# One level of Strassen on the first quarter's value product, with whole weights kept beside the rounded ones and a new order of the work

## The chip, the cores and the metric

The kernel runs on one core of one Trainium2 chip. The metric is the device time of one execution in microseconds (us); the times given are medians over runs. TensorE multiplies matrices (its instructions are called PE below, its weight loads PEld), VectorE (DVE) and ScalarE (ACT) do the elementwise work, and SyncE (SP) issues nearly all transfers between the chip's memory (DRAM) and the on-chip memory.

## The reference

The kernel computes one decoder layer over 2048 tokens of width 1024, in float32. What concerns the change is the cross-attention into 256 memory tokens with 4 heads:

```python
h = rms_norm(x, xa_norm_g[l])
m = rms_norm(mem, mem_norm_g[l])
q = (h @ w_q[l]).reshape(bsz, s, XA_HEADS, XA_HD)
kv = m @ w_kv[l]
k, v = jnp.split(kv, 2, axis=-1)
...
p = jax.nn.softmax(scores, axis=-1).astype(v.dtype)
o = jnp.einsum("bhsm,bmhd->bshd", p, v).reshape(bsz, s, d)
x = x + o @ w_o[l]
```

Before it stand a mixer (an input projection, a gated recurrence, a convolution over 31 positions, an output projection `w_out`), and behind it a feed-forward part with `w_up` and `w_down` and a last norm.

## The kernel before, in words

**Rounded pairs.** Every float32 factor of a large product is split into a rounded part `hi` and a rest `lo` (`split`: ACT writes `hi`, DVE subtracts to get `lo`), and every product is three matmuls of 128 rows by 512 columns (`mm3`: hi·hi, hi·lo, lo·hi) that add up in one PSUM bank.

**Folded memory.** The memory tokens are folded into weights once: `memory_a` makes A (keys times `w_q`, 1024 by 4·256) and `memory_vo` makes VO (values times `w_o`, 4·256 by 1024). Each is written to DRAM as hi and lo (`keep`), in blocks of 128 rows by 512 columns, and later read back block by block (`Rows.get`). So for a token the scores are one product with A and the attention's output is one product of the 1024 probabilities with VO: the latter is the **value product**.

**Quarters.** The tokens go in four quarters of 512. `attend(q)` does quarters 0 and 1 one by one: output projection with `w_out`, scores, softmax, value product (`project_tokens(PT, VO_rows, ...)`: for each half of the output columns, 8 blocks of the probabilities' columns times 4 blocks of 128 tokens, 3 matmuls each). Before the value product the probabilities are turned (128 by 128 transposes on TensorE) and split, into the tiles `pth` and `ptl`. Quarters 2 and 3 are done together by `attend_pair`, whose three products use one level of Strassen's algorithm over 1024 tokens (`Folded`): the left factor is cut into A11, A12 (first 512 tokens, first and second half of the columns) and A21, A22; the weight into B11 to B22; seven products of half the size stand for eight. `Folded.STEPS` lists them. Some use sums: S1 to S4 of the left blocks (made by DVE as they are needed, tiles `s`) and T1 to T4 of the weight's blocks. The T's are made ahead by `fold_weights`, which runs `Folds.prepare` for `w_out`, A and VO in this order and writes them to DRAM (`t_out`, `t_a`, `t_vo`); for A and VO each block is first put together again from its hi and lo by one DVE addition (`wd<-wh,wl`). In `Folded` the split left blocks are the tiles `hidh` and `hidl`, the same names that the feed-forward's down product uses.

**Order.** The program is recorded by Python generators (tasks) that a driver steps by a clock of estimated TensorE time; `TURNS` ranks them, the conditions in `NORMED`, `ATTEND` and `FOLD_AT` gate them, and some thirty numbers (`MIX_WAIT`, `ATT_PACE`, `FOLD_PACE` ...) delay them. `Program.schedule` then orders the recorded instructions of each engine by due times that come from estimated durations and from a transfer rate `DMA_RATE`; on-chip tiles come from 84 slots of 128 by 512 (`SLOTS`), granted in the order of recording. On the chip every engine runs its own list in that fixed order and waits on semaphores, and SP issues its transfers in its list's order. All instructions carry one line (399), so the profile is read by tile names. Of a DRAM tensor the name's number can differ between the two programs (VO_90 and VO_91 are the same tensor).

Of the kernel before, what the change touches and what calls it, by code (L numbers as in the profile page):

```python
# [11 lines left out]
F32 = mybir.dt.float32  # L12
F32R = mybir.dt.float32r
AF = mybir.ActivationFunctionType
ALU = mybir.AluOpType
# [37 lines left out]
DMA_DELAY = 2.5  # L53
DMA_RATE = 300e3
ACT_SWITCH = 1.3
# [367 lines left out]
def hybrid_layer(  # L423
# [519 lines left out]
    def keep(rows, k, half, cols, src):  # L943

        base = (k * 2 + half) * 2
        for i in range(2):
            tok = rows.kept.tok.setdefault(base + i, Buf(None, (1,)))
            pr.dma(rows.kept.at(base + i)[:, cols], src[i].f32(), writes=[tok], join=True)

    def memory_a():  # L950
# [50 lines left out]
        for h in range(4):  # L1001
# [20 lines left out]
    def memory_vo():  # L1022
        yield mem_a
        yield VO_LATE
        for h in range(4):
# [203 lines left out]
    def normed(q, ready, wait):  # L1229
# [6 lines left out]
        mixed[q] = Y, L  # L1236

    def attend(q, ready):
        for t in ready:
# [23 lines left out]

        yield from turned(xs, take)
        turned_x[q].done = True
        yield mem_a
        prob = [[], []]

        def soft(tb, half, p):
            prob[half].append(softmax(p, rp[:, tb : tb + 1], rn[:, tb : tb + 1]))  # L1270

        yield from project_tokens(X, A_rows, soft, None, ATT_PACE[q][1])
        del X
        PT = []
        yield VO_WAIT
        turn_p(prob[0], PT)
        yield mem_vo
        st2 = Stats()

        def add2(tb, half, p):  # L1280
            V("tensor_tensor", xs[tb][half][:], xs[tb][half][:], p[:], op=ALU.add)
            st2.add(tb, half, xs[tb][half][:])
            x2_kept.put((q * NTB + tb) * 2 + half, xs[tb][half][:])

        yield from project_tokens(PT, VO_rows, add2, lambda: turn_p(prob[1], PT), ATT_PACE[q][2])
        attended[q].done = True
        del PT
        r2 = st2.rstd()
# [23 lines left out]
    def combine(name, a, b, op):  # L1312
        t = tmp(name)
        V("tensor_tensor", t[:], a, b, op=op)
        return t
# [322 lines left out]
    class Folds:  # L1638
# [41 lines left out]
    class Folded:  # L1680
# [3 lines left out]

        def __init__(self, src, folds, add):
            self.src, self.folds, self.put, self.s = src, folds, add, {}

# [16 lines left out]
        def gather(self, n):  # L1704
            akey, bkey = self.STEPS[n]
            L, R = [], []
            for i in range(KH):
                src = self.operand(akey, i)
                hi, lo = pair("hid")
# [252 lines left out]
    EARLY, VO_WAIT, V_LATE, Z_COPIED = 5, 2, 500, (0, 1)  # L1962
    MIX_WAIT, MIX_TURN, LN_SUM, LN_SQ, GATES = (5, 7, 6, 0), 5, 6, 0, 3
    MIX_PACE, ATT_PACE = (1, 4, 3, 4), ((0, 3, 0), (0, 2, 2), (6, 3, 3), (5, 9, 0))
    PAUSE, WARM = 2, 16
    FED = ("B21", "T2", "T1", "T3")
    MEM_WAIT, VO_LATE, ATT_TURN, FFN_TURN, X_PACE, T_PACE = 17, 10, 1, (3, 8, 7, 24), 3, 10

    FOLDED = (2, 3)
    PAIR_WAIT, PAIR_TURN, FOLD_PACE = (0, 0, 9, 17), 7, (6, 7, 35)  # L1970
# [4 lines left out]
    NORMED = [lambda: ([m[0]], 108), lambda: ([attended[0]], 31), lambda: ([m[2]], 26), lambda: ([m[3], n[2]], 6)]  # L1975
    ATTEND = [lambda: [n[0]], lambda: [n[1]]]
    TURNS = lambda: [later, first, fold, m[0], mem_a, m[1], first_t, a[0], n[2], m[3], n[0], n[3], mem_vo, n[1], m[2], a[1], a[2], tail]
    X = [HalfX(h) for h in range(NH)]
# [70 lines left out]
```

## Time and profile before

| | |
|---|---|
| median of 3 runs | 2402.87 us (2400.91 to 2404.35) |
| profiled execution: its time / its span | 2401.64 us / 2399.8 us |
| PE / PEld busy | 99% / 82% of the span |
| DVE / ACT busy | 85% / 55% |
| DMA | 604.56 MB, mean 252 GB/s |

A busy PE means that a matmul was in flight; matmuls overlap, so their rate is read from how many start in a stretch. A group's row gives the busy time of its instructions (overlaps counted once) and the mean duration of one; then the idle time of the engine just before them and who ended it.

### The profile page before, as it was taken

How to read it: one execution, taken by the hardware profiler on the slowest of the kernel's cores; microseconds unless marked ns; L12 is line 12 of the kernel's file. 1: busy time of each engine (PE TensorE's matmuls, PEld its weight loads, DVE VectorE, ACT ScalarE, POOL GpSimd, SP SyncE). 2: the span in 40 equal slices, each digit the busy share in tenths (PEclk: the TensorE clock that was granted, in tenths of full speed). 3: DMA queues.
4: the chain of work that ended last, by engine and by line, in shares of the span. 5: the costliest groups of instructions: out<-in, count | busy, mean ns of one | idle time of the engine just before them, and what ended most of it. 6: DMA issues, size and time to landing. Idle time of an engine off the chain costs nothing.

```text
span 2399.8 us, 33427 instructions
## 1 busy us (share of the span) xinstructions
PE 2385.4 (99%) x10940; PEld 1977.0 (82%) x10940; DVE 2034.9 (85%) x3353; ACT 1319.6 (55%) x2380; POOL 0.7 (0%) x6
## 2 busy tenths in 40 slices
PE   9999999999999999999999999999999999999998
PEld 8798888888887888888888888888888888888887
DVE  6999995299899869879999887988988896777787
ACT  7782676357557778695555555554555541222333
POOL 0000000000000000000000000000000000000000
PEclk9999999999999999999999999999999999999999
DMA  9688788775878988787766544556565599887986
GB/s 308 220 297 314 241 298 301 255 263 175 289 261 272 322 275 273 277 284 268 253 231 205 199 171 158 174 177 211 192 215 199 184 308 321 283 280 253 315 299 255
DMA packets 364434, 604.56 MB, mean 252 GB/s; under 512 B 35371, under 2 KB 117547, under 8 KB 364260
## 3 DMA queue, kind: packets, MB, share of 16 engines
q1 hardware_dynamic: 364108, 602.16, 73.3%
q8 instruction: 86, 1.41, 0.2%
q14 instruction: 88, 0.72, 0.1%
q10 hardware_dynamic: 152, 0.28, 0.0%
HBM read 409.36 MB, written 192.94 MB: 251 GB/s over the span
## 4 chain that ended last, share of the span: by engine, by line
PE 84%; DVE 9%; ACT 3%; DMA 2%; issue 1%; SPq 0%; DVEq 0%; ACTq 0%
PE ps L399 84%; DVE conv L399 4%; DMA h<-hid 1%; DMA wl<-w_down 1%; ACT L399 1%; DVE wl L399 1%; DVE hidl L399 0%; DVE s L399 0%; DVE acc L399 0%; ACT gate L399 0%; DVE al L399 0%; ACT junk L399 0%; DMA wl<-w_in 0%; DVE xc L399 0%; DVE xl L399 0%
## 5 line engine op out<-in xcount | busy, mean ns | idle before, releaser
L399 PE MATMUL ps<-Xh,wh 128*128 128x512 f32 x1344 | 523.5, 390 | 0.7 <-ACT u L399 0.7
L399 PE MATMUL ps<-Xh,wl 128*128 128x512 f32 x1344 | 523.4, 389 | 0.7 <-DVE wl L399 0.5
L399 PE MATMUL ps<-Xl,wh 128*128 128x512 f32 x1344 | 523.2, 389 | 0.0
L399 PE MATMUL ps<-wh,hidl 128*128 128x512 f32 x960 | 374.4, 390 | 1.0 <-DVE hidl L399 1.0
L399 PE MATMUL ps<-wh,hidh 128*128 128x512 f32 x960 | 374.5, 390 | 0.8 <-ACT hidh L399 0.8
L399 PE MATMUL ps<-wl,hidh 128*128 128x512 f32 x960 | 373.8, 389 | 0.0
L399 DVE SCALAR_TENSOR_TENSOR conv<-cb,v,conv 128x512 f32<-128x512 f32 x480 | 337.1, 755 | 2.2 <-ACT conv L399 1.4
L399 PEld LDWEIGHTS ps<-Xh,wl 128*128 128x128 f32 x1344 | 252.4, 188 | 53.6 <-DVE wl L399 1.5
L399 PEld LDWEIGHTS ps<-Xh,wh 128*128 128x128 f32 x1344 | 252.4, 188 | 53.1 <-ACT u L399 1.1
L399 PEld LDWEIGHTS ps<-Xl,wh 128*128 128x128 f32 x1344 | 252.4, 188 | 52.4
L399 ACT ACTIVATE hidh<-s 128x512 fp32r<-128x512 f32 x186 | 113.8, 631 | 271.1 <-DVE s L399 232.6
L399 PEld LDWEIGHTS ps<-wh,hidl 128*128 128x128 f32 x960 | 180.3, 188 | 40.2 <-DVE hidl L399 3.1
L399 PEld LDWEIGHTS ps<-wh,hidh 128*128 128x128 f32 x960 | 180.3, 188 | 38.3 <-ACT hidh L399 1.3
L399 PEld LDWEIGHTS ps<-wl,hidh 128*128 128x128 f32 x960 | 180.3, 188 | 37.1
L399 PE MATMUL ps<-xh,wh 128*128 128x512 f32 x512 | 204.6, 400 | 0.5 <-DVE vol L399 0.5
L399 PE MATMUL ps<-xh,wl 128*128 128x512 f32 x512 | 200.4, 391 | 0.0
L399 PE MATMUL ps<-xl,wh 128*128 128x512 f32 x512 | 200.1, 391 | 0.0
L399 ACT ACTIVATE wh<-s 128x512 fp32r<-128x512 f32 x192 | 119.5, 629 | 116.7 <-DVE s L399 82.0
L399 ACT ACTIVATE wh<-raw 128x512 fp32r<-128x512 f32 (+2 forms) x214 | 127.9, 613 | 54.2 <-PE ps L399 22.7
L399 ACT ACTIVATE u<-ps 128x512 f32<-128x512 f32 x144 | 85.7, 595 | 129.1 <-PE ps L399 128.2
L399 DVE TENSOR_TENSOR wl<-raw,wh 128x512 fp32r<-128x512 f32 (+2 forms) x214 | 141.5, 675 | 14.7 <-ACT wh L399 13.7
L399 DVE TENSOR_TENSOR acc<-acc,ps 128x512 f32<-128x512 f32 (+1 forms) x157 | 103.4, 682 | 59.2 <-PE ps L399 55.3
(241 smaller groups left out, 4029.9 us busy)
## 6 DMA issues: line engine op xcount, KB each, us to landing
raw<-in_w_up_dram SPq DMA_DIRECT2D x96, 512.0 KB
wh<-w_down SPq DMA_DIRECT2D x156, 256.0 KB
wl<-w_down SPq DMA_DIRECT2D x156, 256.0 KB
w_down<-wh SPq DMA_DIRECT2D x144, 256.0 KB
w_down<-wl SPq DMA_DIRECT2D x144, 256.0 KB
h<-hid SPq DMA_DIRECT2D x120, 256.0 KB
wh<-w_in SPq DMA_DIRECT2D x96, 256.0 KB
wl<-w_in SPq DMA_DIRECT2D x96, 256.0 KB
```

What stands on the lines that cost most here:

```text
L399: getattr(e, name)(*[resolve(a) for a in args], **{k: resolve(a) for k, a in kw.items()})
```

## The change

1. `attend(0)` does its value product by `Folded` on halves of 256 tokens (`HALVED = ((), (0,))`; the first tuple, for the scores, is empty). The turned probabilities are copied unsplit (tiles `pt`); S1 to S4, the splits and the seven products are 256 tokens wide, with 2 blocks of tokens in place of 4.
2. `memory_a` and `memory_vo` write the whole float32 blocks too (`split_kept`: one more ACT copy, tiles `aw` and `vow`, and one more transfer each, to `A2w` and `VO2w`), and `Folds.block` reads these in place of hi, lo and an addition.
3. `fold_weights` runs VO first, as soon as `memory_vo` is done, then `w_out`, then A.
4. `DMA_RATE` in the planner is 320e3 in place of 300e3, and the numbers that delay and rank the tasks are others.

```diff
-DMA_RATE = 300e3
+DMA_RATE = 320e3
...
+            self.whole = None if w is not None else Kept(name + "w", n * 2, F32)
...
+        tok = rows.whole.tok.setdefault(k * 2 + half, Buf(None, (1,)))
+        pr.dma(rows.whole.at(k * 2 + half)[:, cols], src[2], writes=[tok], join=True)
+
+    def split_kept(name, p):
+        t = *pair(name), tmp(name + "w")
+        split(p[:], *t[:2])
+        ACT(t[2][:], p[:], AF.Copy)
+        return t
...
-                t = pair("a")
-                split(p[:], *t)
+                t = split_kept("a", p)
...
-                t = pair("vo")
-                split(p[:], *t)
+                t = split_kept("vo", p)
...
+    def in_halves(src, kq, tiles):
+        for th in range(2):
+            src[th, kq] = [t[:, th * TT // 2 : (th + 1) * TT // 2] for t in tiles]
...
+        if q in HALVED[1]:
+            src = {}
+
+            def turn_half(half):
+                tiles = []
+                for j in range(4):
+                    p = ps()
+                    with together():
+                        for tb in range(NTB):
+                            transpose(p[:, tb * P : (tb + 1) * P], prob[half][tb][:, j * P : (j + 1) * P], ident[:])
+                    t = tmp("pt")
+                    ACT(t[:], p[:], AF.Copy)
+                    tiles.append(t)
+                in_halves(src, half, tiles)
+
+            turn_half(0)
+            yield mem_vo
+            yield F_vo.done
+
+            def before(n):
+                if n == 1:
+                    turn_half(1)
+                yield 0
+
+            def put(th, tb, half, bank, last):
+                add2(th * NTB // 2 + tb, half, bank, last)
+
+            yield from Folded(src, F_vo, put, TT // 2).run(before, at_once)
+            del src
+        else:
...
-            hi, lo = self.rows.get(k, half)
-            t = tmp("wd")
-            V("tensor_tensor", t[:], hi[:].f32(), lo[:].f32(), op=ALU.add)
-            return t
+            return self.rows.whole.get(k * 2 + half, None, "wd")
...
-            for tb in range(NTB):
+            for tb in range(self.width // P):
...
-        for f, ready, wait in zip((F_out, F_a, F_vo), FOLD_AT(), FOLD_PACE):
+        for f, ready, wait in zip((F_vo, F_out, F_a), FOLD_AT(), FOLD_PACE):
...
-    MIX_WAIT, MIX_TURN, LN_SUM, LN_SQ, GATES = (5, 7, 6, 0), 5, 6, 0, 3
+    MIX_WAIT, MIX_TURN, LN_SUM, LN_SQ, GATES = (4, 3, 2, 0), 9, 6, 0, 3
...
+    HALVED = ((), (0,))
-    FOLD_AT = lambda: ([turned_x[0]], [mem_a, turned_x[1]], [mem_vo])
+    FOLD_AT = lambda: ([mem_vo], [turned_x[0]], [mem_a, turned_x[1]])
```

The lists of the engines show what moves. First DVE at quarter 0's value product. Before, the splits of the turned probabilities (`ptl`) stand among a few sums of the `w_out` fold, and then come the additions of the finished banks to the tokens (`x_...`, one tile for each block of 128 tokens and half of the columns):

```order
L399 TENSOR_TENSOR ptl<-ps,pth 128x512 x4
L399 TENSOR_TENSOR t<-wd 128x512 x2
L399 TENSOR_TENSOR t<-wd,t 128x512 x2
L399 TENSOR_TENSOR ptl<-ps,pth 128x512 x4
L399 TENSOR_TENSOR x_2909<-x_2909,ps 128x512
L399 TENSOR_TENSOR x_2929<-x_2929,ps 128x512
L399 TENSOR_TENSOR x_2946<-x_2946,ps 128x512
```

Now, at the same place, from the splits of A12 (the first row) over the sums of the third product:

```order
L399 TENSOR_TENSOR hidl<-pt,hidh 128x256 x4
L399 TENSOR_TENSOR t<-wd 128x512
L399 TENSOR_TENSOR t<-wd,t 128x512
L399 TENSOR_TENSOR s<-pt 128x256
L399 TENSOR_TENSOR s<-s,pt 128x256
L399 TENSOR_TENSOR x_3035<-x_3035,ps 128x512
L399 TENSOR_TENSOR x_3040<-x_3040,ps 128x512
L399 TENSOR_TENSOR s<-pt 128x256 x2
L399 TENSOR_TENSOR s<-s,pt 128x256 x2
L399 TENSOR_TENSOR hidl<-s,hidh 128x256
```

Sums of 256 columns (`s`), splits of them (`hidl`) and fold sums of `w_out` (`t`) now stand between the additions to the tokens; further down the same list come 16 splits `wl<-t_vo,wh` of the T's.

Next, SP's list inside the value product. Before, it reads VO's hi and lo (`wh`, `wl`), with the fold of `w_out` in between (`wd` read, `t_out` written):

```order
L399 DMA wh<-VO_90 128x512
L399 DMA wl<-VO_90 128x512
L399 DMA wd<-in_w_out_dram 128x512
L399 DMA wh<-VO_90 128x512
L399 DMA wl<-VO_90 128x512
L399 DMA t_out<-t 128x512
L399 DMA wh<-VO_90 128x512
L399 DMA t_out<-t 128x512
```

Now, behind the first two products' blocks:

```order
L399 DMA wl<-VO_91 128x512
L399 DMA wd<-in_w_out_dram 128x512
L399 DMA t_out<-t 128x512 x2
L399 DMA t_vo<-t_vo 128x512 x3
L399 DMA t_out<-t 128x512
L399 DMA x_93<-x_3035 128x512
L399 DMA t_vo<-t_vo 128x512
L399 DMA wd<-in_w_out_dram 128x512 x2
```

The fold of `w_out` is still in between; the T's are read back (`t_vo<-t_vo`), and finished tokens are already written (`x_93`). On PE the place reads, before, with turns of probabilities (`ident,prob`) among the products:

```order
L399 MATMUL ps<-wh,ptl 128x512
L399 MATMUL ps<-ident,prob 128x128 x8
L399 MATMUL ps<-wh,pth 128x512
L399 MATMUL ps<-wl,pth 128x512
L399 MATMUL ps<-wh,ptl 128x512
L399 MATMUL ps<-wh,pth 128x512
```

and now, with all turns ahead and the value product in one piece:

```order
L399 MATMUL ps<-xl,wh 128x512
L399 MATMUL ps<-xh,wl 128x512
L399 MATMUL ps<-ident,prob 128x128 x16
L399 MATMUL ps<-wh,hidh 128x512
L399 MATMUL ps<-wl,hidh 128x512
L399 MATMUL ps<-wh,hidl 128x512
```

From there 168 such matmuls follow each other without another task's work; before there were 192, with 16 turns among them. The last 5833 instructions of PE's list, the feed-forward part, are the same in both programs.

More of the change, by code (lines that the diff above doesn't have):

```diff
@@ L1262, in take, with take_raw @@
             X.append((hi, lo))
-        yield from turned(xs, take)
+        def take_raw(k, p):
+            t = tmp("xa")
+            ACT(t[:], p[:], AF.Copy, scale=vec["v1024"][:, k, G_XA : G_XA + 1])
+            X.append(t)
+        yield from turned(xs, take_raw if q in HALVED[0] else take)
         turned_x[q].done = True
         yield mem_a
-        prob = [[], []]
+        prob = [{}, {}]
         def soft(tb, half, p):
-            prob[half].append(softmax(p, rp[:, tb : tb + 1], rn[:, tb : tb + 1]))
@@ L1272, in attend, with soften @@
-        yield from project_tokens(X, A_rows, soft, None, ATT_PACE[q][1])
+            prob[half][tb] = softmax(p, rp[:, tb : tb + 1], rn[:, tb : tb + 1])
+        if q in HALVED[0]:
+            score = {}
+            def soften(th, tb, half, bank, last):
+                at = (th * NTB // 2 + tb, half)
+                if not last:
+                    t = score[at] = tmp("score")
+                    ACT(t[:], bank[:], AF.Copy)
+                    return
+                t = score.pop(at)
+                V("tensor_tensor", t[:], t[:], bank[:], op=ALU.add)
+                soft(*at, t)
+            yield F_a.done
+            src = {}
+            in_halves(src, 0, X[:KH])
+            in_halves(src, 1, X[KH:])
+            yield from Folded(src, F_a, soften, TT // 2).run(at_once, at_once)
+            del src
+        else:
+            yield from project_tokens(X, A_rows, soft, None, ATT_PACE[q][1])
@@ L1273, in attend, with add2 @@
         del X
-        PT = []
         yield VO_WAIT
-        turn_p(prob[0], PT)
-        yield mem_vo
         st2 = Stats()
-        def add2(tb, half, p):
+        def add2(tb, half, p, last=True):
             V("tensor_tensor", xs[tb][half][:], xs[tb][half][:], p[:], op=ALU.add)
-            st2.add(tb, half, xs[tb][half][:])
-            x2_kept.put((q * NTB + tb) * 2 + half, xs[tb][half][:])
-        yield from project_tokens(PT, VO_rows, add2, lambda: turn_p(prob[1], PT), ATT_PACE[q][2])
+            if last:
+                st2.add(tb, half, xs[tb][half][:])
+                x2_kept.put((q * NTB + tb) * 2 + half, xs[tb][half][:])
@@ new lines, in attend @@
+        if q in HALVED[1]:
+            src = {}
+            def turn_half(half):
[19 more added lines that the diff above has]
+            yield from Folded(src, F_vo, put, TT // 2).run(before, at_once)
+            del src
+        else:
+            PT = []
+            turn_p(prob[0], PT)
+            yield mem_vo
+            yield from project_tokens(PT, VO_rows, add2, lambda: turn_p(prob[1], PT), ATT_PACE[q][2])
+            del PT
@@ L1313, in combine @@
         t = tmp(name)
+        if a.n < TT:
+            t = t[:, : a.n]
         V("tensor_tensor", t[:], a, b, op=op)
@@ L1708, in gather @@
                 src = self.operand(akey, i)
-                hi, lo = pair("hid")
+                hi, lo = (b[:, : self.width] for b in pair("hid"))
                 split(src[:], hi, lo)
```

17 lines of the change are left out of this document (9 added, 8 removed).

## The prediction

> **What bounds the kernel now.** I read the page first, then PE's waits, then stretches of the span. The page:
>
> ```profile
> span 2399.8 us, 33427 instructions
> PE 2385.4 (99%) x10940; PEld 1977.0 (82%) x10940; DVE 2034.9 (85%) x3353; ACT 1319.6 (55%) x2380; POOL 0.7 (0%) x6
> PE 84%; DVE 9%; ACT 3%; DMA 2%; issue 1%; SPq 0%; DVEq 0%; ACTq 0%
> ```
>
> TensorE is in work for 99% of the span, and it carries most of the chain that ended last. Who it waits for:
>
> ```profile
> PE ps L399 <- DMA raw<-in_w_in_dram: 1.6, 1, 1.6
> PE ps L399 <- POOL ident masks.py:199: 1.4, 1, 1.4
> PE ps L399 <- DVE hidl L399: 1.0, 2, 0.6
> PE ps L399 <- DVE xl L399: 0.8, 2, 0.5
> PE ps L399 <- ACT hidh L399: 0.8, 1, 0.8
> PE ps L399 <- ACT u L399: 0.7, 1, 0.7
> PE ps L399 <- DVE wl L399: 0.5, 1, 0.5
> PE ps L399 <- DVE vol L399: 0.5, 1, 0.5
> PE ps L399 <- ACT prob L399: 0.3, 1, 0.3
> ```
>
> These are all: 7.6 us, of which the first two (3.0) belong to the start. So the time is the number of matmuls times the pace at which they start. The pace comes from a stretch that holds nothing but 512-column matmuls, and the quarter's surroundings from the shorter ones (columns: PE, PEld, DVE, ACT, POOL busy with their counts, clock, DMA share, GB/s):
>
> ```profile
> 1600.00:1800.00 200.00, 200.00 (x884) 165.75 (x883) 177.89 (x275) 106.56 (x164) 0.00 (x0) 1.00 0.58 199
> 334.00:436.00 102.00, 102.00 (x498) 85.54 (x498) 63.90 (x116) 52.42 (x124) 0.00 (x0) 1.00 0.91 312
> 380.00:400.00 20.00, 20.00 (x107) 16.90 (x106) 9.54 (x20) 13.22 (x33) 0.00 (x0) 1.00 0.98 336
> 440.00:460.00 20.00, 20.00 (x90) 16.58 (x89) 2.75 (x4) 3.98 (x10) 0.00 (x0) 1.00 0.44 149
> 480.00:500.00 20.00, 20.00 (x96) 16.46 (x95) 18.58 (x29) 9.92 (x16) 0.00 (x0) 1.00 0.98 354
> ```
>
> 200 us / 884 = 0.226 us from one wide matmul to the next, at full clock. Around the first quarter's attention PE has no gap, DVE is much idler than elsewhere, and the transfer engines are nearly full (share 0.91 over 102 us).
>
> **What it removes on PE.** 8 blocks of columns x 2 halves x 4 blocks of tokens x 3 = 192 matmuls become 7 products x 2 blocks of tokens x 4 x 3 = 168, all of the same form. 24 x 0.226 = **5.4 us**, all of it on the path, since PE has no slack to lose here:
>
> ```profile
> L399 PE MATMUL ps<-wh,pth x64: 389/389/477, 423.1 to 467.7; 128*128 128x512 f32 x64
> ```
>
> is the first quarter's value product before. That is 0.23% of 2402.87 us; a measurement of this kernel tells about 0.2% (4.8 us) from no change, so what comes on top decides.
>
> **What it adds on DVE.** One instruction lasts longer than the time to the next. These rows give the durations, and the timeline the pace:
>
> ```profile
> L399 DVE TENSOR_TENSOR t<-wd 128x512 f32<-128x512 f32 x84 | 57.6, 688 | 2.4 <-PE ps L399 1.2 <-DMA wd<-in_w_down_dram 1.1
> L399 DVE TENSOR_TENSOR kvl<-ps,kvh 128x256 fp32r<-128x256 f32 x16 | 6.9, 429 | 0.0
> L399 DVE TENSOR_TENSOR wd<-wh,wl 128x512 f32<-128x512 f32 x32 | 21.8, 689 | 1.3 <-DMA wl<-A 1.3
> L399 DVE TENSOR_TENSOR wl<-t_vo,wh 128x512 fp32r<-128x512 f32 x16 | 10.6, 691 | 0.0
> ```
>
> ```profile
> 205.30 1.29 DVE L399 TENSOR_TENSOR wl<-raw,wh 128x512 fp32r<-128x512 f32 x2
> 206.50 0.68 DVE L399 TENSOR_TENSOR cb<-ps,sg 128x512 f32<-128x512 f32 x1
> ...
> 216.19 0.42 DVE L399 TENSOR_TENSOR kvl<-ps,kvh 128x256 fp32r<-128x256 f32 x1
> 216.52 1.41 DVE L399 SCALAR_TENSOR_TENSOR conv<-cb,v,conv 128x512 f32<-128x512 f32 x2
> ```
>
> Two of 512 columns start 206.50 - 205.30 = 1.20 us ahead of the third: 0.60 each, although one lasts 0.69. One of 256 columns is followed after 0.33, although it lasts 0.42. Over the whole program DVE loses the 32 `wd` sums and 8 `ptl` splits (40 x 0.60 = 24.0) and gains 16 `wl<-t_vo` and 8 additions to the tokens (24 x 0.60 = 14.4), 16 sums `s` and 28 splits `hidl` of 256 columns (44 x 0.33 = 14.5): +4.9 us on an engine with 365 us to spare, so nothing by itself.
>
> What counts is the place. The value product is now one piece of 168 x 0.226 = 38.0 us of PE, and DVE has to deliver to it in the order shown with the change. From the row behind the splits of A12 to the last `wl<-t_vo` that list holds 36 instructions of 512 columns (16 T splits, 12 additions to tokens, 8 `w_out` fold sums) and 36 of 256: 36 x 0.60 + 36 x 0.33 = 33.5 us. It starts late, because the splits of A12 wait for the last turns, a copy and a rounding on ACT:
>
> ```profile
> L399 ACT ACTIVATE pt<-ps 128x512 f32<-128x512 f32 x16 | 8.8, 597 | 3.0 <-PE ps L399 3.0
> L399 ACT ACTIVATE kvh<-ps 128x256 fp32r<-128x256 f32 x16 | 6.1, 379 | 13.2 <-PE ps L399 13.2
> ```
>
> By their busy time a copy takes 8.8 / 16 = 0.55 and a rounding 6.1 / 16 = 0.38: 0.55 + 4 x 0.38 + 0.33 = about 2.4 us (my estimate) behind PE's first value matmul. The third product is the first with a T. Its last `wl` stands 26 instructions down (11 wide, 15 narrow): 2.4 + 6.6 + 5.0 = 14.0 us. PE wants it two products and 10 matmuls in: 58 x 0.226 = 13.1. PE waits 0.9. For the fourth the same count gives 14.0 + 7 x 0.60 + 5 x 0.33 = 19.8 against 14.0 + 24 x 0.226 = 19.4: 0.4 more. From the fifth on, whose weights need no T, DVE is ahead. I take **+1.3 us**. It would be nothing if DVE ran further ahead than this, and with every duration in full (36 x 0.69 + 36 x 0.43 = 40.3) the last weight comes at 42.7, 14 matmuls (3.2) follow, and PE ends 45.9 - 38.0 = 7.9 us late.
>
> [...]
>
> **What it adds on the transfers.** Everything on SP's list between the first read of A for the scores and the last T for the seventh product is 40.9 MB by its sizes; before, up to the last VO block, 32.5 MB. New in it are 16 reads `VO2w`, 16 writes and 16 reads of `t_vo`, less 8 VO reads and what of the `w_out` fold falls behind. Before, the reads came in time with this lead:
>
> ```profile
> L399 SPq DMA_DIRECT2D wh<-A x16: 319/338/872, 334.7 to 394.7; - x16
> L399 PE MATMUL ps<-wh,xah x64: 389/389/477, 357.8 to 415.2; 128*128 128x512 f32 x64
> L399 SPq DMA_DIRECT2D wh<-VO x16: 320/382/1467, 405.2 to 435.8; - x16
> L399 PE MATMUL ps<-ident,xn 128*128 128x128 f32 x192 | 22.1, 273 | 0.0
> ```
>
> The first A block is asked for 357.8 - 334.7 = 23.1 us ahead of its use. With that lead, 246 wide matmuls and 64 turns (22.1 / 192 = 0.115 each) to the value product, its seventh product starts 23.1 + 55.6 + 7.4 + 144 x 0.226 = 118.6 us after that request and wants its last T split at 120.9. The transfers need 40.9 MB / 336 GB/s = 121.7, and the split about 1.3: late by 2.1 us. At 354 GB/s, the other full stretch, they need 115.5 and are in time. PE's list now has 18 matmuls of VO's making ahead of the scores that stood among them before, and SP's list doesn't, so the lead should be 4 us longer: I take **nothing**, with 0 to 2.1 as the near bounds.
>
> [...]
>
> **The rest.** The 32 additional ACT copies `aw` and `vow` (0.55 each, as `pt` above) hold a PSUM bank a little longer while A and VO are made; ACT is 55% busy, and PE has other tasks' matmuls there: nothing, up to 32 x 0.55 = 17.6 if each were waited for. ACT loads its tables 71 times instead of 81 by its list:
>
> ```profile
> L399 ACT ACT_TABLE_LOAD x81 | 103.9, 1283 | 21.8 <-DVE smalls L399 14.6 <-DMA raw<-in_w_in_dram 4.5 <-DVE gate L399 1.3
> ```
>
> 13 us less on an engine that PE waits for 1.8 us in all. The new order rewrites the places of the waits on `xl`, `vol` and `prob` (1.6 us together). I take half as gone, **-0.8**; it could be all, or as much again on top. The feed-forward part's order on PE is unchanged, so its waits (`hidl`, `hidh`, `u`, `wl`: 3.0) stay.
>
> **Sum.** On the profiled execution: 2401.64 - 5.4 + 1.3 - 0.8 = 2396.7. That execution lies 1.2 us under the median, so against medians: **2397.9 us**. Its own range is 2395 to 2401.
>
> **Rivals.**
>
> *More than the slots come back (0.20).* With DVE ahead, and the 1.6 us and half of the feed-forward's 3.0 gone: 2402.9 - 5.4 - 3.1 = 2394.4. For it: fewer table loads, and less to read for the folds. Against it: the unchanged list of the second half.
>
> *DVE sets the pace of the value product (0.10).* Durations count in full: 2402.9 - 5.4 + 7.9 = 2405.4, within 0.2%. For it: the sums S, their splits and the T's form chains with ACT, and a waiting instruction holds all behind it in DVE's list, the additions that free PSUM banks too. Against it: the timeline above.
>
> *The transfers come late: slower (0.17).* If they move the 312 GB/s of the stretch 334 to 436, 40.9 MB take 131.1; with the split and the old lead PE waits 131.1 + 1.3 - 120.9 = 11.5 us: 2409.0. It eats up the saving below 40.9 MB / (120.9 - 1.3 + 5.4 us) = 327 GB/s. For it: no other PE work stands in the 168 matmuls to fill a wait, and `t_vo` must be written before it is read. Against it: at 312 the share was 0.91 and not full, and the 440 to 460 stretch, at 0.44, shows the queue running empty soon behind.
>
> *The new order costs elsewhere: slower (0.05).* Banks held by the copies `aw` and `vow` while A and VO are made, each waited for: 2402.9 - 4.9 + 17.6 = 2415.6; it decides from 9.7 us on, a little over half of that. Against it: PE waits for no such copy now, though every block already has one (`ah`, `voh`).
>
> That the change doesn't do what it says is excluded: PE's list has 24 matmuls less.
>
> **How the numbers follow.** The forecast has 0.48. Its 2397.9 lies just beyond the 0.2% bound (2398.1), so a little over half of it, 0.27, counts as faster; with the first rival 0.47. Within 0.2%: the other 0.21 and the DVE rival's 0.10: 0.31. Slower: both last rivals, 0.22. The range goes from 2392 (the first rival, all waits but the start's gone: 2402.9 - 5.4 - 4.6 = 2392.9, less the spread of runs) to 2409; about 0.15 lies outside.
>
> **What would show it right or wrong.** In the changed kernel's profile PE should have 24 matmuls less at 0.226 us. In the stretch of the first `hidh` matmuls the waits on `wl` or `hidl` should be about 1 us together; over 5 us with DVE full is the DVE rival, waits with `t_vo` or VO transfers behind them and a share over 0.95 are the transfer rival. Waits in the first 250 us would be the last one. The forecast is wrong if PE's waits outside the start and the feed-forward part come to more than 4 us, or if the feed-forward part itself has changed its time.

## The result: 20 us slower, and the profile after

The changed kernel takes 2423.06 us (median of 4 runs, 2419.76 to 2424.86) against 2402.7 of the kernel before (2400.91 to 2404.35): ratio 1.0083, 95% interval 1.007 to 1.0096. I had forecast 2397.9 and a range up to 2409. The profiled execution is 2424.86 us long, 23.2 more than the one of before. Its page:

```profile
span 2423.1 us, 33586 instructions
PE 2393.0 (99%) x10916; PEld 1975.8 (82%) x10916; DVE 2044.9 (84%) x3381; ACT 1338.7 (55%) x2446; POOL 0.7 (0%) x6
PE 80%; DVE 9%; ACT 5%; DMA 4%; issue 2%; SPq 0%; DVEq 0%; ACTq 0%
```

The 24 matmuls are gone (10,940 to 10,916), and PE still fills 99% of the span: the share of busy time hides the loss, the chain of waits shows it (PE 84% before, now 80%; ACT and DMA both up by 2). PE's own waits come first (us in total, times, longest):

```profile
PE ps L399 <- DMA raw<-in_w_kv_dram: 5.0, 1, 5.0
PE ps L399 <- ACT wh L399: 3.1, 2, 2.1
PE ps L399 <- DMA raw<-in_w_in_dram: 2.9, 1, 2.9
PE ps L399 <- ACT mem L399: 2.1, 1, 2.1
PE ps L399 <- DVE wl L399: 1.3, 6, 0.2
PE ps L399 <- DVE xl L399: 1.2, 4, 0.3
PE ps L399 <- DVE ptl L399: 1.1, 1, 1.1
```

The first two rows weren't there before. All waits together are 22.4 us, 14.8 more than before, too few for 23 us more. So I add up something that sees more: the time from each matmul's start to the next one's, less the median of this time for matmuls of the same tiles and form. I call this sum the **loss**; it is read from one profiled execution of each kernel. It comes to 20.7 us before and 48.2 after: +27.5, against which stand the 24 x 0.226 = 5.4 us saved; with 0.5 behind the last matmul that is 22.6 of the span's 23.3. By stretches of the span:

| us of the span | before | after | more |
|---|---|---|---|
| 0 to 100 (start) | 7.8 | 10.0 | 2.2 |
| 100 to 200 (A is made) | 1.0 | 10.7 | 9.7 |
| 400 to 500 (value product) | 0.1 | 9.5 | 9.4 |
| 500 to 600 (convolution of a later quarter) | 1.8 | 6.1 | 4.3 |
| 600 to 800 | 2.9 | 4.9 | 2.0 |
| 1000 to 1100 (start of the feed-forward part) | 0.0 | 2.5 | 2.5 |
| all others | 7.1 | 4.5 | -2.6 |

**While A is made.** SP's timeline (start, duration, and how many issues in a row):

```profile
164.61 0.43 SPq L399 DMA_DIRECT2D A2w<-aw  x1
165.14 0.85 SPq L399 DMA_DIRECT2D A<-al  x2
166.09 0.98 SPq L399 DMA_DIRECT2D A<-ah  x2
167.51 1.40 SPq L399 DMA_DIRECT2D A2w<-aw  x2
169.44 1.96 SPq L399 DMA_DIRECT2D A<-al  x2
171.49 1.24 SPq L399 DMA_DIRECT2D raw<-in_w_kv_dram  x2
```

and PE's at that place:

```profile
171.35 0.28 PE L399 MATMUL ps<-kvh,qtl 128*128 128x256 f32 x1
176.61 1.62 PE L399 MATMUL ps<-mt,raw 128*128 128x256 f32 x3 [4.97 <-DMA raw<-in_w_kv_dram]
```

The w_kv blocks that PE needs at 171.4 us are asked for at 171.49, behind stores. Between 157 and 171.45 us SP issues 24 transfers; they take it 10.2 us, 0.42 each in the median. By the trace 16 of the new half-block writes `A2w<-aw` stand ahead of this read. (The expectations below say 28, and 30 for g1_old_numbers: these are the writes ahead of a later w_kv read, at 205 us.) In the kernel before, the same two reads stand among the stores, go out 9 to 12 us earlier and come in time:

```profile
158.98 0.90 SPq L399 DMA_DIRECT2D A<-al  x2
159.97 0.42 SPq L399 DMA_DIRECT2D raw<-in_w_kv_dram  x1
160.48 0.96 SPq L399 DMA_DIRECT2D A<-ah  x2
161.54 1.01 SPq L399 DMA_DIRECT2D A<-al  x2
162.63 0.45 SPq L399 DMA_DIRECT2D raw<-in_w_kv_dram  x1
```

The hole itself loses 5.1 us, and what follows it another 2.9 (columns: PE, PEld, DVE, ACT, POOL busy with counts, granted clock, DMA share, GB/s):

```profile
168.00:172.00 4.00, 3.63 (x31) 3.43 (x29) 3.34 (x7) 2.96 (x9) 0.00 (x0) 1.00 0.77 265
172.00:176.00 4.00, 0.00 (x0) 0.00 (x0) 3.64 (x8) 3.81 (x7) 0.00 (x0) 0.95 0.88 267
178.00:182.00 4.00, 4.00 (x11) 3.17 (x10) 2.98 (x5) 1.84 (x4) 0.00 (x0) 0.50 0.97 347
182.00:184.00 2.00, 2.00 (x15) 1.78 (x14) 0.00 (x0) 0.37 (x1) 0.00 (x0) 0.90 0.83 290
```

From 175.6 to 182.4 us the granted clock is half, and PE is "busy" all the same.

**The value product.** From the first matmul of its 168 to the first one behind them it takes 47.0 us, 8.9 over 168 x 0.2265. The main hole is at the third product. ACT and DVE there, one fence each:

```profile
450.19 0.63 ACT L399 ACTIVATE wh<-t_vo 128x512 fp32r<-128x512 f32 x1 [0.58 <-DMA t_vo<-t_vo]
450.73 1.01 ACT L399 ACTIVATE hidh<-s 128x256 fp32r<-128x256 f32 x3
453.18 0.63 ACT L399 ACTIVATE junk<-x 128x512 f32<-128x512 f32 x1 [0.85 <-DVE x L399]
453.81 0.61 ACT L399 ACTIVATE wh<-t_vo 128x512 fp32r<-128x512 f32 x1
```

```profile
451.46 1.09 DVE L399 TENSOR_TENSOR hidl<-s,hidh 128x256 fp32r<-128x256 f32 x3
452.47 0.68 DVE L399 TENSOR_TENSOR x<-x,ps 128x512 f32<-128x512 f32 x1
454.46 0.69 DVE L399 TENSOR_TENSOR wl<-t_vo,wh 128x512 fp32r<-128x512 f32 x1 [0.97 <-ACT wh L399]
```

```profile
451.93 0.40 PE L399 MATMUL ps<-wh,hidl 128*128 128x512 f32 x1
454.48 0.50 PE L399 MATMUL ps<-wh,hidh 128*128 128x512 f32 x1 [2.15 <-ACT wh L399]
```

Read backwards: PE waits 2.15 us for the fourth T of the product; ACT rounds it at 453.81, behind a square (`junk`) that waits for an addition to the tokens; DVE makes this addition at 452.47, behind three splits for the *next* product. Neither DVE nor the transfers are full around the hole: from 450 to 460 us DVE is busy for 7.60 us, at a DMA share of 0.77 (columns as above).

```profile
450.00:460.00 10.00, 7.39 (x22) 4.76 (x21) 7.60 (x15) 5.52 (x12) 0.00 (x0) 0.83 0.77 252
```

### The profile page after: what moved, and what is told of

Its sections match the earlier page's. It is cut to its first block, busy times and chain, and to the rows that moved or that the text cites. A ratio compares the mean times of both kernels' runs of the same rounds, so it can differ in the third digit from the quotient of the medians.

```text
span 2423.1 us, 33586 instructions
## 1 busy us (share of the span) xinstructions
PE 2393.0 (99%) x10916; PEld 1975.8 (82%) x10916; DVE 2044.9 (84%) x3381; ACT 1338.7 (55%) x2446; POOL 0.7 (0%) x6
## 4 chain that ended last, share of the span: by engine, by line
PE 80%; DVE 9%; ACT 5%; DMA 4%; issue 2%; SPq 0%; DVEq 0%; ACTq 0%
PE ps L399 80%; DVE conv L399 4%; ACT gate L399 1%; DVE gate L399 1%; ACT L399 1%; ACT junk L399 1%; DVE wl L399 1%; DVE xc L399 1%; DMA wh<-w_down 0%; DMA raw<-in_w_out_dram 0%; DMA wl<-w_in 0%; DMA xn<-xn 0%; DVE x L399 0%; DMA wl<-w_down 0%; SPq L399 0%
## 5 line engine op out<-in xcount | busy, mean ns | idle before, releaser
L399 PE MATMUL ps<-wh,hidh 128*128 128x512 f32 x1016 | 397.5, 391 | 2.7 <-ACT wh L399 2.1
L399 PE MATMUL ps<-wl,hidh 128*128 128x512 f32 x1016 | 396.9, 391 | 0.9 <-DVE wl L399 0.8
L399 PE MATMUL ps<-wh,hidl 128*128 128x512 f32 x1016 | 396.6, 390 | 0.6 <-DVE hidl L399 0.6
L399 ACT ACTIVATE hidh<-s 128x512 fp32r<-128x512 f32 (+1 forms) x202 | 120.5, 614 | 289.1 <-DVE s L399 219.8
L399 PEld LDWEIGHTS ps<-wh,hidh 128*128 128x128 f32 x1016 | 191.1, 188 | 44.2 <-ACT wh L399 3.3
L399 PEld LDWEIGHTS ps<-wl,hidh 128*128 128x128 f32 x1016 | 191.2, 188 | 43.2 <-DVE wl L399 3.8
L399 PEld LDWEIGHTS ps<-wh,hidl 128*128 128x128 f32 x1016 | 191.0, 188 | 41.7 <-DVE hidl L399 2.3
L399 ACT ACTIVATE wh<-raw 128x512 fp32r<-128x512 f32 (+2 forms) x214 | 127.3, 614 | 58.6 <-PE ps L399 23.3
L399 DVE TENSOR_TENSOR wl<-s,wh 128x512 fp32r<-128x512 f32 x192 | 130.1, 685 | 18.6 <-ACT wh L399 14.0
```

The source lines that it names most:

```text
L399: getattr(e, name)(*[resolve(a) for a in args], **{k: resolve(a) for k, a in kw.items()})
```

## The experiments

The theory after the result: the saving is real, and the loss is made by lists that are worked in order, first SP's, then those of ACT and DVE. Rivals: the new numbers of the order lose the time whatever the structure; the bytes and copies of the whole blocks do; the narrow product is too dense for DVE and ACT in any order.

All values in one place (loss in us by stretch; "piece": what the value product's 168 matmuls take over 168 x 0.2265). Ratios are to the kernel before, run beside them on the same chip (its medians 2402.4 to 2403.14):

| run | us | ratio (95%) | 100-200 | 400-500 | 500-600 | 600-800 | 1000-1100 | piece |
|---|---|---|---|---|---|---|---|---|
| before | 2402.7 | 1 | 1.0 | 0.1 | 1.8 | 2.9 | 0.0 | |
| after | 2423.06 | 1.0083 (1.007-1.0096) | 10.7 | 9.5 | 6.1 | 4.9 | 2.5 | 8.9 |
| g1_no_strassen | 2423.27 | 1.0084 (1.0069-1.0099) | 6.4 | 0.1 | 5.3 | 9.2 | 2.4 | |
| g1_old_numbers | 2512.04 | 1.0455 (1.0439-1.047) | 8.5 | 0.4 | 28.2 | 74.8 | 0.0 | 19.5 |
| g1_new_numbers | 2432.9 | 1.0126 (1.0111-1.0141) | 2.1 | 0.1 | 2.8 | 30.3 | 2.6 | |
| g1_rate | 2407.95 | 1.0021 (1.0012-1.0031) | 2.1 | 0.1 | 2.2 | 4.3 | 1.4 | |
| g2_writes_pool | 2415.31 | 1.0052 (1.0037-1.0067) | 3.6 | 9.0 | 5.5 | 5.0 | 2.4 | 8.8 |
| g2_t_reads_pool | 2424.01 | 1.0089 (1.0074-1.0104) | 8.5 | 12.4 | 4.9 | 4.9 | 2.4 | 12.1 |
| g2_both_pool | 2419.48 | 1.0069 (1.0054-1.0084) | 3.1 | 10.7 | 6.3 | 4.9 | 2.8 | 10.2 |
| g2_no_whole_a | 2415.38 | 1.0057 (1.004-1.0073) | 2.0 | 8.5 | 4.0 | 5.7 | 2.7 | 8.2 |
| g3_no_t_reads | 2420.02 | 1.0067 (1.005-1.0083) | 8.7 | 7.5 | 4.2 | 5.9 | 2.7 | 7.2 |
| g3_no_sums | 2420.51 | 1.007 (1.0055-1.0085) | 8.1 | 8.6 | 5.6 | 4.9 | 2.9 | 8.4 |
| g3_neither_writes_pool | 2413.52 | 1.0045 (1.003-1.006) | 3.2 | 5.4 | 5.2 | 5.2 | 2.4 | 5.0 |
| g3_a_fold_before | 2416.77 | 1.0057 (1.0042-1.0072) | 1.1 | 8.4 | 4.7 | 5.5 | 2.4 | 8.2 |
| g4_squares_off | 2412.09 | 1.0042 (1.0027-1.0057) | 3.3 | 3.2 | 4.9 | 5.0 | 3.1 | 2.9 |
| g4_squares_later | 2416.6 | 1.0058 (1.0043-1.0073) | 3.8 | 8.2 | 4.3 | 5.7 | 2.4 | 8.0 |
| g4_issue_cost | 2416.48 | 1.0057 (1.0042-1.0072) | 8.6 | 8.8 | 5.7 | 5.7 | 2.3 | 8.9 |
| g4_pool_planned | 2419.8 | 1.0069 (1.0053-1.0086) | 3.2 | 8.0 | 4.0 | 5.7 | 2.4 | 7.9 |
| g5_no_fold_sums | 2429.49 | 1.0111 (1.0094-1.0128) | 6.4 | 16.7 | 6.1 | 4.8 | 2.6 | 16.6 |
| g5_all_off | 2417.21 | 1.0059 (1.0044-1.0074) | 5.5 | 9.9 | 4.7 | 4.9 | 2.8 | 7.9 |

Where a kernel's lists are untouched up to 200 us (the changed kernel, g2_t_reads_pool, g3_no_t_reads, g3_no_sums, g5_no_fold_sums), the loss between 100 and 200 reads 6.4 to 10.7. So a difference in one stretch says something from about 4 us on.

### Structure or numbers

g1_no_strassen:

```diff
-    HALVED = ((), (0,))
+    HALVED = ((), ())
```

> The changed kernel with the first quarter's value product as one plain product again (192 matmuls instead of 168); whole weights, the rate of transfers and all numbers of the order stay. Theory (most of the loss comes from reads that stand behind stores in SP's list, and from TensorE's half clock behind each such wait): the 24 matmuls come back (+5.4 us), the reads of T during the value product are gone, and with them what that piece of 45.8 us has over 168 x 0.226 = 38.0 (-7.8); the wait of 5 us at 171 us stays, since 28 writes of whole A blocks still stand ahead of the w_kv reads: about 2421 us, 1.007 of the kernel before. Rival 1 (the narrow value product is too dense for DVE and ACT, and it carries most of the loss): about 2405, 1.001. Rival 2 (the numbers of the order lose the time wherever they are used): 2423 + 5.4 = about 2428.

Measured 2423.27, within 0.2 us of the changed kernel. The plain product's 192 matmuls lose 0.1 us, its wide ones run as before. So the Strassen piece costs 8.9 to save 5.4, about 3.5 us net. The total doesn't show it: between 600 and 800 us this plan loses 4.3 more. The loss at A's making stays: 6.4, the low end of what unchanged lists show.

g1_old_numbers and g1_new_numbers exchange the block of constants (paces, turns, rates), for instance

```diff
-    MIX_WAIT, MIX_TURN, LN_SUM, LN_SQ, GATES = (4, 3, 2, 0), 9, 6, 0, 3
+    MIX_WAIT, MIX_TURN, LN_SUM, LN_SQ, GATES = (5, 7, 6, 0), 5, 6, 0, 3
```

> The changed kernel's structure (value product by Strassen, whole weights kept, the folds in the changed order) with the numbers of the order and the rate of transfers of the kernel before. 30 writes of whole A blocks stand ahead of the w_kv reads in SP's list here too. Theory (the queue): the wait at about 171 us and the half clock behind it stay, 8 to 9 us, the value product again waits for T: 2412 to 2425 us, 1.004 to 1.009 of the kernel before. Rival 2 (the new numbers lose the time): with the old numbers the saving of 5.4 us shows, about 2398, 0.998.

> The kernel before, its structure untouched, with the changed kernel's numbers of the order and its rate of transfers (its three paces of folds in the order that fits its three folds). Theory (the queue): no whole weights are written, so nothing is put ahead of the w_kv reads, and there is no T to wait for: 2400 to 2408 us, 1.000 to 1.002 of the kernel before. Rival 2 (the numbers): most of the loss is here too, 2415 us or more, 1.005 or more.

> The kernel before with one number changed, the rate of transfers that its planner assumes (300 to 320 GB/s). It shows how far the time scatters when only the plan is laid out anew. Theory (the queue): within 3 us of 2402.7, since stores and reads keep their mixture. Rival 2 (any plan laid out anew, without its numbers tuned to it, loses some ten us): 2410 or more, 1.003 or more.

Old numbers on the new structure, 2512, miss what both theories said. My transfer of them was unlucky: VO's fold kept its old pace of 35 while the first quarter now waits for this fold, so its value product comes at 692.8 instead of 438.3 us. Of the 109 us, 98 are lost between 500 and 800 us; that the late value product makes them is my reading, which no run tests. Two readings stay good: A's making loses 8.5 with the old numbers too, and the value product is worse (19.5) than with the new. New numbers on the old structure cost 30 us, as the rival has it by the total, but not where it has them: nearly all lies (27.4) between 600 and 800, and next to nothing in the two stretches where the changed kernel loses most. Changing the one rate costs 4.9 us, between the two expectations. So a plan laid out anew scatters by some us by itself, and the numbers belong to a structure; but the losses at 171 us and in the value product are there with both sets of numbers when the structure is the new one, and with neither when it is the old one. The 2.5 us at the start of the feed-forward part go with the numbers: 2.6 with them on the old structure, 0.0 without them on the new.

### SP's list

In these four runs the plan is the changed kernel's, each engine's order untouched; only the issuing queue differs, or something is left out as the program is written out.

```diff
-                e = self.engines[o.on]
+                e = self.engines[o.via or o.on]
...
-        pr.dma(rows.whole.at(k * 2 + half)[:, cols], src[2], writes=[tok], join=True)
+        pr.dma(rows.whole.at(k * 2 + half)[:, cols], src[2], writes=[tok], join=True, via="Pool")
```

> The changed kernel, every engine's order as it is, but the 48 writes of whole blocks (32 of A, 16 of VO) issued from GpSimd's queue instead of SP's. Theory (the queue): the wait of 5.0 us for the w_kv read at 171 us and the half clock behind it, 9.7 of the 10.7 us lost between 100 and 200 us, go; the value product stays as it is: about 2414 us, 0.996 of the changed kernel. Rival (the bytes of the whole blocks or the additional ACT copies hold up A's making, not SP's order): the writes move the same bytes, so 2421 us or more, with the loss between 100 and 200 us still over 7.

Measured 2415.31: 7.8 us less than the changed kernel. The w_kv read now goes out at 163.44 us (171.49 in the changed kernel), and PE's waits have

```profile
PE ps L399 <- ACT wh L399: 3.1, 2, 2.1
PE ps L399 <- DVE wl L399: 1.7, 7, 0.3
PE ps L399 <- DMA raw<-in_w_kv_dram: 0.4, 1, 0.4
```

The value product is unchanged (piece 8.8).

```diff
+                if o.skip:
+                    continue
...
+        pr.ops[-1].skip = name == "a"        # the copy aw
+        pr.ops[-1].skip = rows is A_rows     # the write A2w
```

> The changed kernel, order as it is, with the whole blocks of A left out: neither the 16 copies on ACT nor the 32 writes of 128 KB are made, and the folds that read the whole blocks read A's upper parts in their place (so the combined weights of A miss their lower parts). Theory (the queue): as with the writes on the other queue, about 2414 us; if it comes out within 2 us of that kernel, the copies on ACT and the bytes cost nothing of their own. Rival (copies and bytes): clearly below it, by 5 us or more.

2415.38: as with the writes on the other queue. The 16 copies of A on ACT and the 4 MB cost nothing of their own that could be told apart; the place in SP's list was the price. The same bytes issued from another engine's queue are worth 7.8 us (2423.06 to 2415.31; 4.5 between the next two runs, 2424.01 to 2419.48), because what stands behind an issue in the list waits too, at about 0.42 us for each.

```diff
-            pr.dma((b[:] if shape is None else flat(b)).f32(), self.at(i), reads=[self.tok[i]])
+            pr.dma((b[:] if shape is None else flat(b)).f32(), self.at(i), reads=[self.tok[i]], via="Pool" if self.name == "t_vo" else None)
```

> The changed kernel, every engine's order as it is, but the 16 reads of T in the first quarter's value product issued from GpSimd's queue instead of SP's. Theory (the queue): T is read as soon as it is written, the 4 waits of ACT for it (4.5 us) and the half clock behind PE's 2.3 us wait go, the value product takes 38 to 40 us instead of 45.8, the loss between 400 and 500 us falls from 9.5 to under 3: about 2416 us. Rival (DVE and ACT themselves are too slow for the dense piece): the piece stays over 43 us, 2421 us or more.

> Both: whole-block writes and the reads of T from GpSimd's queue, the changed kernel's order otherwise as it is. Theory (the queue): the two gains add up, 2423.1 - 9 - 7 = about 2407 us; what is left over the kernel before less 5.4 us is the start (+2), the stretch of 500 to 600 us (+4) and that at 1085 us (+2.5). Rival: 2420 us or more.

A miss: 2424.01 alone (it also moves the 16 T reads of a later pair of quarters), and 2419.48 with the writes, 4.2 *more* than with the writes alone. What GpSimd's queue waited for before the reads of T, and how long they took to land:

```profile
L399 POOL DMA_DIRECT2D t_vo<-t_vo x16: 536/536/678, 439.4 to 472.7; - x16
  PE ps L399: 12.0, 4
  DVE hidl L399: 8.1, 3
DMA to landing us min/median/max: 3.3/5.0/7.2
```

On GpSimd's queue the reads don't stand behind SP's other issues any more, and they are held up all the same, by PE and DVE. I take it that they wait for a free block of SBUF, which these two give back; no run tests that. My theory for this stretch falls: SP's list alone doesn't make its loss.

### Inside the value product

Again the order is the changed kernel's; here work is left out.

```diff
+            if narrow:
+                read.skip = True          # no read of T; the splits take a block that is always there
```

> The changed kernel, order as it is, with the 16 reads of T in the first quarter's value product left out; ACT and DVE make the same 32 splits, but from a block that lies in SBUF all along (so that quarter's T weights are constants). Theory A (the reads of T, wherever they are issued, come too late): the four waits of ACT for T (4.5 us) go, PE's 2.3 us wait and the half clock behind it too, the loss between 400 and 500 us falls from 9.5 to under 3: about 2416 us. Theory B (the round trips between ACT and DVE, each working its list in order, are what is late; the reads only look like it): the loss between 400 and 500 us stays over 7, about 2422 us.

```diff
+                if self.width < TT:
+                    for o in pr.ops[count:]:
+                        o.skip = True     # the sums S1 to S4; the splits take A12's halves
```

> The changed kernel, order as it is, with the 16 sums of tokens (S1 to S4, 256 columns, on DVE) of the first quarter's value product left out; the splits read the halves of A12 in place of the sums. Theory A (reads of T late): little changes, the loss between 400 and 500 us stays over 7, 2420 us or more. Theory B (round trips): DVE has 16 x 0.33 = 5.3 us less to do there and ACT's waits for the sums (10.3 us in all) go; the loss falls under 4, about 2417 us.

> Both left out, reads of T and sums, and the whole-block writes issued from GpSimd's queue as in the earlier run (2415.3 us). If the value product's loss is made by either or by both, the loss between 400 and 500 us falls under 2 and the time to 2415.3 - 8 = about 2407 us; what is left over 2402.4 - 5.4 = 2397 then lies in the start, in the stretch of 500 to 600 us and at 1085 us (about 8 us). Rival (something else in that stretch, the additions to the tokens or the w_out fold's sums on DVE): over 2411 us.

Each alone does little (piece 8.9 to 7.2 and to 8.4), both together leave 5.0. Neither theory had it so: with one cause taken away, the next one in the lists is as late. A hole of 1.7 us (1.57 of it a wait for ACT) stays at the same fourth T of the third product, behind the square shown above.

```diff
+                if q in HALVED[1]:
+                    name, args, kw = pr.ops[-1].calls[0]
+                    pr.ops[-1].calls[0] = (name, (args[0], donor[:], args[2]), kw)
```

> As the last run but one (reads of T and sums of tokens left out, whole-block writes on GpSimd's queue: 2413.5 us, loss between 400 and 500 us 5.4), and the 8 squares on ACT for the norm behind the first quarter's value product read a block that lies in SBUF all along in place of the updated tokens, so that they wait for no addition on DVE. Theory (a loop through the lists: the last T split of a product stands behind a square, the square behind an addition, the addition behind splits of the next product): the 1.7 us wait at the third product goes, the loss falls under 3, the time to about 2411 us. Rival (DVE and ACT are simply too slow there): the loss stays at 5 or more, 2413 us or more.

2412.09, and the piece is down to 2.9, with the same squares still made: only what they wait for has changed. The matmuls `wh,hidh`, from the start of the first to the start of the last, now read

```profile
L401 PE MATMUL ps<-wh,hidh x56: 388/389/495, 434.2 to 474.5; 128*128 128x512 f32 x56
```

against

```profile
L399 PE MATMUL ps<-wh,hidh x56: 388/389/628, 438.3 to 483.9; 128*128 128x512 f32 x56
```

in the changed kernel: 40.3 us instead of 45.6. So 6 of the 8.9 us hang on these three things together. The kernel's time shows 3.2 of them (2415.31 to 2412.09); in the profiled executions the start and the stretch at 1000 us lose 2.3 more. A complete kernel can't leave them out, but it can move the squares:

```diff
+        for o in [o for o in order if o.late]:
+            ...                           # each square behind the next four ACT instructions
```

> The changed kernel complete, with the whole-block writes on GpSimd's queue (2415.3 us alone) and, in ACT's list, each of the 8 squares of the first quarter's value product moved behind the next four instructions; all else in its order. Theory (loop through the lists): the loss between 400 and 500 us falls from 9.0 to 6 or 7, 2412 to 2413 us. Rival: no change, 2415 us.

No change within the scatter (2416.6 against 2415.31; piece 8.0 against 8.8). The traces show why: the third product's loss falls from 4.9 to 2.3, and the fourth's rises from 1.1 to 4.6. There PE waits 1.65 us for ACT's rounding of a T. In ACT's list this stands behind the rounding of a sum of tokens, and for that sum ACT waits 1.93 us. So the square was a link of the chain, and with it moved the next link is as late. In every run that keeps this product whole it costs 7.9 us or more over its matmuls. Whether another order of the lists could feed it in time, no run shows.

### Other plans, and what stays open

g3_a_fold_before gives up A's whole blocks (VO's stay, A's folds add hi and lo on DVE again); g4_issue_cost changes one number of the planner, g4_pool_planned has it count the writes on GpSimd:

```diff
-ISSUE = dict(SP=0.1, ACT=0.3, Pool=1.0)
+ISSUE = dict(SP=0.42, ACT=0.3, Pool=1.0)
```

> The changed kernel with A's whole blocks gone for good: A's folds read the upper and lower parts and add them on DVE as in the kernel before; VO's whole blocks, Strassen in the value product, and all numbers of the order stay; the plan is laid out anew. Theory (SP's list): without the 32 writes the w_kv reads come in time, the loss between 100 and 200 us falls under 3, and the time to about 2414 us, if the new plan costs nothing elsewhere. Rival (a plan laid out anew scatters by more than that): any other place loses 5 us or more, 2419 us or more although the loss between 100 and 200 us is gone.

> The changed kernel with one number of its planner changed: 0.42 us in place of 0.1 for an issue on SP's queue; the plan is laid out anew. In the new list 13 instead of 28 writes of whole A blocks stand ahead of the w_kv read that was late. Theory (SP's list, and a planner that doesn't see its cost): the loss between 100 and 200 us falls from 10.7 to about 4, about 2416 us, if nothing else gets worse. Rival (any plan laid out anew scatters): other places lose more than is gained, 2420 us or more.

> The changed kernel with the 48 whole-block writes on GpSimd's queue from the start, so that the planner counts them there; the plan is laid out anew. Theory: as with the writes moved after planning, about 2415 us. Rival (scatter of a new plan): over 2420 us although the loss between 100 and 200 us is under 4.

2416.77, 2416.48 and 2419.8. Without the writes A's making is as before (1.1). With an issue priced at about what it takes (0.42), the w_kv reads go out at 156.71 and 162.41 us, with 10 and 13 whole-block writes ahead of them instead of 16, but another read is late instead (`wl<-w_in`, 2.1 us), so the stretch keeps 8.6. With the writes planned on GpSimd the stretch is cured (3.2), and 200 to 300 loses 7.4 instead of 1.1, which I put down to the scatter of a new plan.

```diff
+                for o in t.ops:
+                    if o.eng == "DVE" and o.calls[0][1][0].buf is t:
+                        o.skip = True     # the w_out fold's sums; the write takes a block of w_out
```

> The changed kernel, order as it is, with the 16 sums of the w_out fold on DVE left out (16 x 0.60 = 9.6 us; the writes take a block of w_out in their place, so the later quarters' combined w_out weights are plain blocks). Half of these sums stand in the value product's stretch, half behind it. Theory (the order of the folds moved this work from a stretch in which DVE was idle into one in which it is the last): the loss between 500 and 600 us falls from 6.1 under 3, the one between 400 and 500 from 9.5 to about 8: 2418 us or less. Rival (the stretch of 500 to 600 us is short of DVE for other reasons): its loss stays over 5, 2421 us or more.

> All together: whole-block writes on GpSimd's queue; reads of T, sums of tokens and the w_out fold's sums left out; the squares independent of the updated tokens. If these are the causes, the losses of 100 to 200, 400 to 500 and 500 to 600 us come to less than 7 together (26.3 in the changed kernel, 2.9 in the kernel before): 2407 us or less. Rival (causes are missing): 2411 us or more.

Both are slower than what they started from, though they do less work: a fault of the experiment. Each write now holds a block of `w_out` until it has read it, and the blocks are of one pool. ACT's waits between 434 and 490 us in g5_no_fold_sums:

```profile
ACT hidh L401 <- DMA t_out<-wd: 5.4, 1, 5.4
ACT wh L401 <- DMA t_vo<-t_vo: 4.6, 2, 3.7
```

A rounding waits 5.4 us for the block of a write that has nothing to do with it. The stretch of 500 to 600 us kept 6.1. So its cause stays open: DVE is busy for 99.1 of these 100 us before and for 99.6 after, and whether the w_out fold's later place pushes it over is not decided. No version that beat the kernel before came out of these runs; the best complete one is g2_writes_pool, 1.0052.

## Why the prediction was wrong

Two steps failed, and they carry 19 of the 27.5 us of new loss: the feeding of the value product was priced at 1.3 us, and the writes of the whole blocks on SP's list weren't priced at all.

- **What it removes**: right. 24 matmuls less, at the same 0.2265 us; the saving is in the span, under 27.5 us of new loss.
- **What it adds on DVE** is the first failed step: +1.3 forecast, 8.9 measured. I counted how long DVE's list takes at its pace, and took each entry as ready when its turn came. The place was right: the third product, for which 0.9 was forecast, lost 5.4, of which 2.3 in the hole at its last T, 1.5 at half clock behind it and 1.5 in small waits. Its last `wl` starts 16.1 us behind the first value matmul, where my count had it done at 14.0. What I left out is that ACT's list is in the chain too: T's rounding stands behind a square, that behind an addition, that behind splits of the next product. That DVE is ahead from the fifth product on failed as well: the last three products lost 2.4. The rival on DVE named chains with ACT in its favour, but its 7.9 came from durations in full, and DVE was busy for 7.60 of the 10 us around the hole and not full. That 7.9 lies near 8.9 is luck.
- **Transfers** nothing at the value product: not contradicted. Around the hole the DMA share was 0.77 and not full, and without any read of T the piece still lost 7.2. From 460 to 480 us the share was 0.96 to 1.05, so for the 2.1 us that products four to six lost there the rate isn't excluded. The rates that bounded this term were too narrow a choice: "the other full stretch" at 354 GB/s was not the only other one. In the profile before, stretches of 20 us with a share of 0.95 or more move 313 to 406 GB/s.
- **The rest** holds the second failed step. I priced the 32 copies on ACT (nothing; for the 16 of A g2_no_whole_a bears it out) and forgot what follows them: 32 writes of A on SP's list, 16 of them ahead of reads that PE then waits for, at about 0.42 us each. The stretch lost 9.7 us more; with the writes on another queue the kernel gains 7.8. I had followed SP's queue only where the value product reads. The rival on the new order has its place right ("Waits in the first 250 us") and its mechanism wrong (PSUM banks held by copies).
- **Waits on xl, vol and prob, -0.8, and the feed-forward part unchanged**: wrong. The first quarter's piece was not the only thing laid out anew; 500 to 600, 600 to 800 and 1000 to 1100 us lost 8.8 more, of which the runs trace the last 2.5 to the numbers and leave the other 6.3 open, as they do the start's 2.2.
- **The price of a wait**: I counted a wait as its own length. Behind the two large ones the half clock and what goes with it add 1.5 and 2.9 us (below).

## What to carry to other kernels

Where an engine works its list in order, sum not only its work but follow the last-needed entry back through every list it crosses, and for an added store ask which reads stand behind it in the issuing queue. A step that saves a few tenths of a per cent on the bound engine (5.4 us here) can be lost when its feeding needs three engines in turn within a few matmuls (8.9 us here). When an experiment leaves work out, look at what then holds the buffers.

## What the runs showed of the hardware

Behind some holes PE's granted clock is 0.50 for 3.4 us, or for 6.8, and the hole can be as short as 0.49 us. The four spells in the changed kernel (starts at 52.7, 175.6, 455.5 and 557.9 us) come to 17 us, so by my estimate up to 8.5 us are lost; a fifth, of 6.8 us, lies in its start, at 8.3 us. The kernel before has none behind its start until its last microseconds. Behind the 2.15 us wait of the value product, and at 558 us:

```profile
452.00:454.00 2.00, 0.33 (x2) 0.00 (x0) 1.49 (x4) 1.15 (x4) 0.00 (x0) 1.00 0.86 271
456.00:458.00 2.00, 2.00 (x6) 1.58 (x5) 1.81 (x4) 1.73 (x4) 0.00 (x0) 0.50 0.60 230
556.00:558.00 2.00, 1.51 (x19) 1.40 (x19) 1.74 (x4) 2.00 (x5) 0.00 (x0) 0.96 0.45 172
558.00:560.00 2.00, 2.00 (x6) 1.52 (x6) 2.00 (x5) 1.98 (x6) 0.00 (x0) 0.50 0.03 8
```

At half clock a 512-column matmul starts 0.43 us behind the one before it, at full clock 0.2265. At 558 us PE waited only 0.49 us, but between 24 tiny ones:

```profile
555.47 1.15 PE L399 MATMUL ps<-ident,raw 4*128 4x4 f32 x16
557.11 0.65 PE L399 MATMUL ps<-ident,raw 4*128 4x4 f32 x8 [0.49 <-DVE v L399]
557.69 0.67 PE L399 MATMUL ps<-xh,wh 128*128 128x512 f32 x1
```

So a wait of 2.15 us, and a stretch of tiny matmuls with one of 0.49, have a spell behind them. The length of the wait alone doesn't decide: behind 1.60 us in the kernel before (for `raw<-in_w_in_dram`, until 7.49 us) and 1.07 us in the changed one (for `ptl`, until 782.5 us) the granted clock stays at 1.00.
